# A decoder block in split float32: low parts a megabyte at a time, and the high-weight products first

## The chip, the core and the metric

The kernel runs on one core of a Trainium2 chip. A core has a matrix engine (TensorE, PE in the profile), a vector engine (VectorE, DVE), an activation engine (ScalarE, ACT), a general engine (GpSimd, POOL), and a queue engine (SyncE, SP) that issues the transfers; 16 DMA engines move data between the device memory and the on-chip memory. Matmul results land in accumulator banks, each 128 rows of 512 floats. The engines run apart from each other, each in the order of its own list, and meet at semaphores.

The metric is the device time of one execution in microseconds. The kernel before takes 1417.61 us (median of three runs, 1417.16 to 1417.9).

## The reference

One block of a decoder over 256 tokens of width 2048, in float32:

```
h    = rmsnorm(x, attn_norm_w)
proj = h @ w_in            # rq rk rv rg | mq mk mv | g_ret g_moba
o_ret  = retention(rotary(rq), rotary(rk), rv)     # 4 heads of 256, chunks of 128
o_ret  = silu(rg) * norm(o_ret) * ret_norm_w
o_moba = moba_attention(rotary(mq), rotary(mk), mv) # 8 heads of 128
merged = sigmoid(g_ret) * (o_ret @ w_ret_up) + sigmoid(g_moba) * (o_moba @ w_moba_up)
x  = x + merged @ w_out
h2 = rmsnorm(x, ffn_norm_w)
a, b = split(causal_conv3(h2 @ w_ffn_up))           # 2 x 5632 wide
x  = x + (silu(a) * b) @ w_ffn_down
out = rmsnorm(x, final_norm_w)
```

Nearly all of the work is in the products with weights.

## The kernel before, in words

**Numbers in two parts.** To be exact enough, each operand of a product is split into a high part, which is the number rounded to the format in which TensorE multiplies, and a low part, which is the rest. ScalarE writes the high part (L185, a copy that rounds), VectorE the low part (L186, the number less its high part). A product is then three matmuls: high by high, high by low and low by high (`mm3`, L196 to L199; every matmul is recorded by `mm`, L194).

**Slots.** The weights, some 264 MB, stream through the chip in halves of 512 KB (128 x 1024 floats, `raw`), each fetched by one transfer (`load`, L168) into one of RAW_BUFS = 4 buffers, and split by `part` into `whi` and `wlo`, PART_BUFS = 4 buffers each. Two halves are a slot, and there are 252 slots, numbered from 0 in the order in which TensorE goes through them: keys, queries, values and gates of the two attentions (0 to 55), the gates and the up products of both attentions, four columns of blocks with 12 slots each (56 to 103), the output product (104 to 119), the up projection of the feed-forward part (120 to 207) and its down projection in two passes of 22 slots (208 to 251).

**Three kinds of slot.** Keys, queries and the up projection are *wide*: the weights stand in the array and the tokens move through; a slot is 16 matmuls of 512 columns (high and low part of the tokens side by side, by the high part of the weights) and 16 of 256 columns (by the low part), in two rounds of two blocks of columns for keys, queries and the first up slots and in one round for the rest. The others are *plain*: 24 matmuls of 512 columns, three for each of eight products, or *seven*: a Strassen form with 21, in which four sums of weight blocks (VectorE) replace a product. Sums of token blocks for the seven slots are made by `seven_sums`: L748 to L752 on VectorE, a copy on ScalarE (L755), and the low part (L756). The tables SEVEN_GATES, SEVEN_OUT and SEVEN say which slots of a stage are seven slots.

**The order of the work.** There is no scheduler: the program is written slot by slot, and each engine's list is the order of the writing. At a slot: first the split of the next slot's weights (`part`, or the seven form), and with it the load of the slot that will use the freed buffers; then `seven_sums` where there is one; then one step of each task in hand (`run_tasks`: rotary, attention, gates, convolution, gathering of results); then the slot's matmuls (`issue`, L204), with the small matmuls and transposes of the tasks put into the middle of the stream. So what a task on VectorE or ScalarE needs stands in line behind the split of the next slot's weights.

**Places that the prediction names.** L629 is the gate of the retention attention, which reads an accumulator, on ScalarE; L846 multiplies products with the gates, from accumulators, on VectorE; L851 adds the output product to x (VectorE), which is then transposed on TensorE (L202) for the up projection; L541 is the convolution, L545 the silu `g` behind it (ScalarE) and L546 the product with the other branch. In the down projection `seven_parts` (first pass, sums written in place) and `seven_parts_apart` (second pass, sums in tiles `tt`, their parts in `th`, `tl` or `t`) split a seven slot.

Of the kernel before, what the change touches and what calls it, by code (L numbers as in the profile page):

```python
# [33 lines left out]
RAW_BUFS, PART_BUFS = 4, 4  # L34
# [45 lines left out]
SEVEN = ((4, 7, 10, 13, 16, 18), (3, 5, 7, 9, 12, 14, 16))  # L80
# [45 lines left out]
def block(ctx: ExitStack, tc: tile.TileContext, a):  # L126
# [15 lines left out]
    def f32(ap):  # L142
        return ap.bitcast(F32)
# [15 lines left out]
    def spans(n):  # L159
        step = CW if n < 1 else 2 * CW  # L160
        return [slice(c, c + step) for c in range(0, 2 * CW, step)]

    def load(n, *some):
        if n < n_halves:
            if n not in raws:
                raws[n] = wp.tile([P, 2 * CW], F32, name="raw", bufs=RAW_BUFS)
            for w in some or spans(n):
                nc.sync.dma_start(raws[n][:, w], wts[order[n], :, w])  # L168

    def part(n, *some):  # L170

        if n < n_halves:
            if n not in parts:
                parts[n] = [wp.tile([P, 2 * CW], F32R, name=x, bufs=PART_BUFS) for x in ("whi", "wlo")]
            for w in some or spans(n):
# [20 lines left out]
    def mm3(out, ah, al, bh, bl, start, stop, **kw):  # L196
        mm(out, ah, bh, start=start, stop=False, **kw)
        mm(out, ah, bl, start=False, stop=False, **kw)
        mm(out, al, bh, start=False, stop=stop, **kw)  # L199

# [72 lines left out]
    xtiles = [px.tile([P, 2, 2, S], F32R, name=f"xb{i}", bufs=1) for i in range(KD // 2)]  # L273
# [18 lines left out]
    def part_x(k):  # L292
        for j in range(k, min(k + 2, KD)):
            split2(xh[j], xl[j], xts[j // 4][:, j % 4, :], vec[:, V_ATTN + j:V_ATTN + j + 1])
            if k == 0:
                part(0, spans(0)[j])
# [230 lines left out]
    def ffn(acc, f):  # L527

        pf = big["pf"]
        u = big["u"][f % 2]  # L530
        y = pf.tile([P, 2, S], F32, name="y", bufs=2)
# [12 lines left out]
        g = pf.tile([P, S], F32, name="g", bufs=2)  # L544
# [72 lines left out]
    def closed(kind, n, acc, more):  # L617
# [17 lines left out]
        elif kind == "up":  # L635
            if n == 0:
# [4 lines left out]
                big["u"] = [pf.tile([P, 2, S + 2], F32, name=f"u{i}") for i in range(2)]  # L641
# [14 lines left out]
    load(0)  # L656
# [8 lines left out]
    part(1)  # L665
# [12 lines left out]
    def seven_parts(n):  # L678


        r, q = raws.pop(n), raws.pop(n + 1)
        b11, b21, b12, b22 = r[:, :CW], r[:, CW:], q[:, :CW], q[:, CW:]
        (h1, l1), (h2, l2) = [[wp.tile([P, 2 * CW], F32R, name=x, bufs=PART_BUFS) for x in ("whi", "wlo")]
                              for _ in range(2)]
        (h3, l3), t2 = big["t14"], big["t2"]
# [15 lines left out]
        for i in (0, 1):  # L701
            load(n + i + RAW_BUFS)
# [490 lines left out]
```

## Time and profile before

| | before |
|---|---|
| time, median of 3 runs | 1417.61 us |
| the profiled execution, first to last instruction (span) | 1415.7 us |
| TensorE busy | 1405.6 us (99%) |
| VectorE busy | 1103.4 us (78%) |
| ScalarE busy | 776.9 us (55%) |
| read from memory | 272.86 MB, 194 GB/s over the span |
| granted TensorE clock | 0.999 |

The span is measured inside the profiled execution; the times of the runs are some 2 us longer, since they hold what lies around it. In the timeline a row gives start, duration, engine, line, operation, what is written from what, and the shape; rows of the same kind that follow each other are joined (x2). Matmuls are pipelined: a row of 0.39 us may be followed by the next 0.23 us later, so the pace is read from starts, not from durations.

The chain that ended last has next to nothing in it: the last operations of the kernel and 0.3% of the span in which nothing was waited for.

### The profile page before, as it was taken

How to read it: one execution, taken by the hardware profiler on the slowest of the kernel's cores; microseconds unless marked ns; L12 is line 12 of the kernel's file. 1: busy time of each engine (PE TensorE's matmuls, PEld its weight loads, DVE VectorE, ACT ScalarE, POOL GpSimd, SP SyncE). 2: the span in 40 equal slices, each digit the busy share in tenths (PEclk: the TensorE clock that was granted, in tenths of full speed). 3: DMA queues.
4: the chain of work that ended last, by engine and by line, in shares of the span. 5: the costliest groups of instructions: out<-in, count | busy, mean ns of one | idle time of the engine just before them, and what ended most of it. 6: DMA issues, size and time to landing. Idle time of an engine off the chain costs nothing. (4 is left out here: it accounts for less than half of the span.)

```text
span 1415.7 us, 19297 instructions
## 1 busy us (share of the span) xinstructions
PE 1405.6 (99%) x7215; PEld 1202.7 (85%) x7215; DVE 1103.4 (78%) x1512; ACT 776.9 (55%) x1043; POOL 5.6 (0%) x14
## 2 busy tenths in 40 slices
PE   9999999999999999999999999999999999999997
PEld 7888888888888888888888888888888888888886
DVE  6687656867888989798677777777777778998886
ACT  6555454545556555555565555555555555555553
POOL 0000000000000000000000000000000000000000
PEclk9999999999999999999999999999999999999999
DMA  8755555555656656577555656556556555657664
GB/s 296 260 187 168 167 186 172 178 179 172 212 182 209 195 191 209 180 236 238 167 190 188 197 181 193 194 182 194 191 182 196 189 179 178 207 180 236 191 217 160
DMA packets 77325, 276.22 MB, mean 195 GB/s; under 512 B 8720, under 2 KB 9776, under 8 KB 77232
## 3 DMA queue, kind: packets, MB, share of 16 engines
q1 hardware_dynamic: 76800, 274.20, 60.1%
q8 instruction: 56, 0.92, 0.3%
q10 hardware_dynamic: 432, 0.79, 0.2%
q14 instruction: 37, 0.30, 0.1%
HBM read 272.86 MB, written 2.10 MB: 194 GB/s over the span
## 5 line engine op out<-in xcount | busy, mean ns | idle before, releaser
L186 DVE TENSOR_TENSOR wlo<-raw,whi 128x1024 fp32r<-128x1024 f32 (+1 forms) x493 | 584.1, 1219 | 234.7 <-ACT whi L185 108.8
L185 ACT ACTIVATE whi<-raw 128x1024 fp32r<-128x1024 f32 (+1 forms) x493 | 514.5, 1058 | 458.9 <-PE acc L194 247.9
L194 PE MATMUL acc<-xb,whi 128*128 128x512 f32 x1920 | 466.0, 392 | 1.1 <-ACT whi L185 1.1
L194 PEld LDWEIGHTS acc<-xb,whi 128*128 128x128 f32 x1920 | 350.6, 188 | 68.6 <-ACT whi L185 2.1
L194 PEld LDWEIGHTS acc<-xb,wlo 128*128 128x128 f32 x1920 | 250.9, 191 | 12.2
L194 PE MATMUL acc<-xb,wlo 128*128 128x256 f32 x1920 | 254.6, 282 | 0.0
L194 PE MATMUL acc<-whi,xb 128*128 128x512 f32 x572 | 183.3, 391 | 0.0
L194 PEld LDWEIGHTS acc<-whi,xb 128*128 128x128 f32 x572 | 107.4, 188 | 22.1
L194 PE MATMUL acc<-wlo,xb 128*128 128x512 f32 x286 | 111.5, 390 | 0.0
L194 PE MATMUL acc<-wlo,gh 128*128 128x512 f32 (+1 forms) x226 | 87.5, 387 | 0.0
L194 PE MATMUL acc<-whi,gl 128*128 128x512 f32 (+1 forms) x226 | 87.5, 387 | 0.0
L194 PE MATMUL acc<-whi,gh 128*128 128x512 f32 (+1 forms) x226 | 87.5, 387 | 0.0
L541 DVE SCALAR_TENSOR_TENSOR y<-u,vec,y 128x256 f32<-128x256 f32 x176 | 73.5, 479 | 0.0
L194 PEld LDWEIGHTS acc<-wlo,xb 128*128 128x128 f32 x286 | 53.7, 188 | 10.6
L194 PE MATMUL z<-whi,xb 128*128 128x512 f32 x156 | 51.9, 390 | 0.0
L194 PEld LDWEIGHTS acc<-wlo,gh 128*128 128x128 f32 x226 | 42.4, 188 | 8.8
L194 PEld LDWEIGHTS acc<-whi,gh 128*128 128x128 f32 x226 | 42.4, 188 | 8.7
L194 PEld LDWEIGHTS acc<-whi,gl 128*128 128x128 f32 x226 | 42.4, 188 | 8.6
L538 ACT ACTIVATE y<-u,vec 128x256 f32<-128x256 f32 x88 | 47.7, 590 | 0.0
L194 PEld LDWEIGHTS z<-whi,xb 128*128 128x128 f32 x156 | 29.3, 188 | 6.1
L755 ACT ACTIVATE s<-room 128x512 fp32r<-128x512 f32 x13 | 8.2, 633 | 44.7 <-DVE room L752 44.7
L534 DVE TENSOR_TENSOR u<-y,r2b 128x512 f32<-128x512 f32 x44 | 30.5, 693 | 1.5
(304 smaller groups left out, 1593.1 us busy)
## 6 DMA issues: line engine op xcount, KB each, us to landing
raw<-in_wts SPq DMA_DIRECT2D x503, 512.0 KB, 4.3
rows<-in_x SPq DMA_DIRECT2D x4, 512.0 KB, 7.7
x<-in_x SPq DMA_DIRECT2D x4, 512.0 KB, 6.1
xt<-in_xT SPq DMA_DIRECT2D x3, 512.0 KB, 7.0
wf<-in_wf SPq DMA_DIRECT2D x2, 512.0 KB, 7.1
out<-x SPq DMA_DIRECT2D x4, 256.0 KB, 2.5
out<-x ACTq DMA_DIRECT2D x2, 384.0 KB, 3.3
xt<-in_xT SPq DMA_DIRECT2D x2, 256.0 KB, 4.4
```

The costliest lines, as they stand in the source:

```text
L185: nc.scalar.activation(hi, full, AF.Copy)
L186: nc.vector.tensor_sub(lo, full, f32(hi))
L194: to.append(lambda: nc.tensor.matmul(out, a, b, **kw))
L534: nc.vector.tensor_mul(u[:, :, 2:], y, twice(big["r2b"]))
L538: nc.scalar.activation(y[:, j, :], u[:, j, 0:S], AF.Identity, scale=cv[j][:, 0:1], bias=cv[j][:, 3:4])
L541: nc.vector.scalar_tensor_tensor(y[:, j, :], u[:, j, i:i + S], cv[j][:, i:i + 1], y[:, j, :], op0=OP.mult, op1=OP.add)
L755: nc.scalar.activation(hi, sums, AF.Copy)
```

## The change

1. **Buffers of a slot.** `raw`, `whi` and `wlo` become tiles of a whole slot (128 x 2048), two of each. ScalarE still writes the high parts in two copies of 128 x 1024, but VectorE makes the low parts of the slot in one operation (`part`). Both loads of the slot after next go out when that operation is done. The first three slots are still split half by half (`part_of`).
2. **Order within a slot.** In plain and seven slots `all3` writes first, for every product, high by high and low by high, the two that use the high part of the weights; then, for every product, the one that uses their low part.
3. **One form of the seven slots.** `seven_parts` replaces both old forms. Another variant of the Strassen form is used, with other signs and another order of products; the four sums are made ahead, three of them in `tt`; one subtraction of 128 x 2048 makes the low parts of the slot, and one of 128 x 1536 those of the three sums. In the down projection `tt` lies in a tile `uy` which also holds the up projection's u, y and g of the last tasks. The first seven slot of the first pass moves from the fifth to the sixth place (SEVEN 4 to 5: slot 212 to 213).
4. **Keys and queries** are described as going in two halves of a slot with two blocks of columns each; the calls of `wide_products` have other text and the same arguments for every slot.

```diff
-RAW_BUFS, PART_BUFS = 4, 4
+RAW_BUFS, PART_BUFS = 2, 2
...
-SEVEN = ((4, 7, 10, 13, 16, 18), (3, 5, 7, 9, 12, 14, 16))
+SEVEN = ((5, 7, 10, 13, 16, 18), (3, 5, 7, 9, 12, 14, 16))
...
-    def part(n, *some):
-
-        if n < n_halves:
-            if n not in parts:
-                parts[n] = [wp.tile([P, 2 * CW], F32R, name=x, bufs=PART_BUFS) for x in ("whi", "wlo")]
-            for w in some or spans(n):
-                split2(parts[n][0][:, w], parts[n][1][:, w], raws[n][:, w])
-            if not some or some[0] == spans(n)[-1]:
-                raws.pop(n)
-                load(n + RAW_BUFS)
...
+    def loads(s):
+        raws.pop(s)
+        for h in range(2):
+            load(2 * (s + RAW_BUFS) + h)
...
+    def part(s):
+
+        if 2 * s < n_halves:
+            hi, lo = parts[s] = part_tiles()
+            for h in range(2):
+                w = slice(2 * CW * h, 2 * CW * (h + 1))
+                nc.scalar.activation(hi[:, w], raws[s][:, w], AF.Copy)
+            nc.vector.tensor_sub(lo, raws[s], f32(hi))
+            loads(s)
...
+    def all3(products):
+
+        for bank, edges, ah, al, bh, bl in products:
+            for x in (ah, al):
+                begin, end = edges(1)
+                mm(bank, x, bh, start=begin, stop=end, to=stream)
+        for bank, edges, ah, al, bh, bl in products:
+            begin, end = edges(1)
+            mm(bank, ah, bl, start=begin, stop=end, to=stream)
...
+                uy = big["uy"] = pf.tile([P, 8 * S + 2 * S + 8], F32, name="uy")
+                y1, u1, u0, y0, g = [uy[:, w:w + n] for w, n in ((0, 2 * S), (2 * S, 2 * S + 4), (4 * S + 4, 2 * S + 4),
+                                                                 (6 * S + 8, 2 * S), (8 * S + 8, 2 * S))]
...
+    def seven_parts(s, tt, th, tl):
+
+        r = raws[s]
+        b11, b21, b12, b22 = [r[:, x * CW:(x + 1) * CW] for x in range(4)]
+        hi, lo = parts[s] = part_tiles()
+        nc.vector.tensor_sub(tt[0], b22, b21)
+        nc.vector.tensor_sub(b22, b22, b12)
+        nc.vector.tensor_sub(tt[1], b12, tt[0])
+        nc.vector.tensor_sub(tt[2], b11, tt[1])
+        for h in range(2):
+            w = slice(2 * CW * h, 2 * CW * (h + 1))
+            nc.scalar.activation(hi[:, w], r[:, w], AF.Copy)
...
+            full = tt[3]
+            nc.scalar.activation(th, full, AF.Copy)
+            nc.vector.tensor_sub(lo, r, f32(hi))
+            nc.vector.tensor_sub(tl, full, f32(th))
+        loads(s)
...
-        for key, (ah, al), (bh, bl) in (
-                ("e0", a(0, 0), b(0, 0)), ((0, 0), a(0, 1), b(0, 1)), ((0, 1), ss[3], b(1, 1)),
-                ("e3", ss[2], b(1, 0)), ("e2", ss[1], t2), ("e1", ss[0], t1), ((1, 0), a(1, 1), t4)):
-            begin, end = accs.edges(key, 3)
-            mm3(accs.bank(key), ah, al, bh, bl, begin, end, to=stream)
+        all3([(accs.bank(key), functools.partial(accs.edges, key), *x, *y) for key, x, y in (
+            ("e0", a(0, 1), b(0, 1)), ((0, 0), a(0, 0), b(0, 0)), ((0, 1), ss[3], b(1, 0)), ("e3", ss[2], b(1, 1)),
+            ("e1", ss[0], t1), ("e2", ss[1], t2), ((1, 0), a(1, 0), t4))])
...
+        full = big["uy"][:, 4 * S + 4:4 * S + 4 + 3 * CW].rearrange("p (x t) -> p x t", x=3)
+        tt = three(full) + [full]
...
-            elif slot < 3:
+            if slot < 3:
                 for h in range(2):
                     wide_products(accs, 4 * kc + 2 * h, halves[h:h + 1], nk, range(4))
             else:
-                for blocks in ((0, 1), (2, 3)):
+                for blocks in (range(4),) if kind == "up" and n > 0 else ((0, 1), (2, 3)):
                     wide_products(accs, 4 * kc, halves, nk, blocks)
```

What this does to the engines' lists, at the three places of which the prediction speaks. First TensorE at slot 56, the first slot of the gates stage; xb is the token block, acc an accumulator. Before, its beginning:

```order
L194 MATMUL acc<-whi,xb_80 128x512
L194 MATMUL acc<-wlo,xb_80 128x512
L194 MATMUL acc<-whi,xb_80 128x512 x2
L194 MATMUL acc<-wlo,xb_80 128x512
L194 MATMUL acc<-whi,xb_80 128x512 x2
```

and now the whole slot:

```order
L215 MATMUL acc<-whi,xb_80 128x512 x16
L215 MATMUL acc<-wlo,xb_80 128x512 x8
```

The eight matmuls with the low part of the weights moved from every third place to the end, and the slot's second accumulator, with which its twelfth matmul (counted from 0) used to begin, is now begun by its eighth.

Second VectorE around the same slot: the split of slot 56, the token sums (L748 to L756 before, L773 to L781 now), and the split of slot 57. Before:

```order
L186 TENSOR_TENSOR wlo<-raw,whi 128x1024 x2
L748 TENSOR_TENSOR room<-xb_80 128x512
L749 TENSOR_TENSOR room<-room 128x128
L750 TENSOR_TENSOR room<-room 128x128
L751 TENSOR_TENSOR room<-room 128x128
L752 TENSOR_TENSOR room<-room 128x128
L756 TENSOR_TENSOR s_3194<-room,s_3194 128x512
L186 TENSOR_TENSOR wlo<-raw,whi 128x1024 x2
```

and now:

```order
L196 TENSOR_TENSOR wlo<-raw,whi 128x2048
L773 TENSOR_TENSOR room<-xb_80 128x512
L774 TENSOR_TENSOR room<-room 128x128
L775 TENSOR_TENSOR room<-room 128x128
L776 TENSOR_TENSOR room<-room 128x128
L777 TENSOR_TENSOR room<-room 128x128
L781 TENSOR_TENSOR s_2966<-room,s_2966 128x512
L196 TENSOR_TENSOR wlo<-raw,whi 128x2048
```

The list is the same but for the two operations that became one ahead of the sums and behind them. Slot 120, the first of the up projection, has the same exchange ahead of the four additions of L851, and its matmuls keep their order.

Third VectorE from the split of slot 212 to that of slot 215, now (gl is the low part of the activations, L583 the convolution, L588 the product behind the silu, t the low parts of the sums):

```order
L196 TENSOR_TENSOR wlo<-raw,whi 128x2048
L207 TENSOR_TENSOR gl<-uy,gh 128x256
L583 SCALAR_TENSOR_TENSOR uy<-uy,vec 128x256 x4
L729 TENSOR_TENSOR uy<-raw 128x512
L730 TENSOR_TENSOR raw<-raw 128x512
L731 TENSOR_TENSOR uy<-raw,uy 128x512
L732 TENSOR_TENSOR uy<-raw,uy 128x512
L745 TENSOR_TENSOR wlo<-raw,whi 128x2048
L746 TENSOR_TENSOR t<-uy,t 128x1536
L588 TENSOR_TENSOR uy<-uy 128x256
L196 TENSOR_TENSOR wlo<-raw,whi 128x2048
L773 TENSOR_TENSOR room<-otrh,otrl 128x512
```

Before, the convolution stood behind the split of the first seven slot (212), and the split of slot 213 and the sums followed it. Now it stands ahead of the first seven split (213); that split's sums are written into the tile uy, which the silu behind the convolution writes too, and the sums of tokens follow with slot 214.

More of the change, by code (lines that the diff above doesn't have):

```diff
@@ L1 @@
+import functools
 from contextlib import ExitStack
@@ L199, in mm3, with counted, edges @@
         mm(out, al, bh, start=False, stop=stop, **kw)
+    def counted(n):
+        left = [n]
+        def edges(some):
+            begin = left[0] == n
+            left[0] -= some
+            return begin, left[0] == 0
+        return edges
+    def all3(products):
[6 more added lines that the diff above has]
+            mm(bank, ah, bl, start=begin, stop=end, to=stream)
     def flip(out, full):
@@ L727, in two_blocks, with three @@
+    def three(tile, w=CW):
+        return [tile[:, x, :] for x in range(3)]
     def two_blocks(k, kind="dn"):
@@ L780, in plain_products @@
                 w = slice(kk * CW, (kk + 1) * CW)
[L781 to L784 removed]
+                some += [(accs.bank((t, j)), functools.partial(accs.edges, (t, j)),
+                          *(x[:, kk, t * P:(t + 1) * P] for x in xs), hi[:, w], lo[:, w]) for t in range(NT)]
+        all3(some)
     class Banks:
@@ L902, in middle_slots @@
                 middle_pool()
-                t124 = [[big[x][:, i, :] for x in ("th", "tl")] for i in range(3)]
-            n = 2 * (slot + 1)
+                th, tl = big["th"], big["tl"]
+                t124 = list(zip(three(th), three(tl)))
             if q == 0 and seven:
@@ L946, in middle_slots @@
             run_tasks()
-            halves = [parts.pop(2 * slot + h) for h in range(2)]
+            halves = halves_of(slot)
             if seven:
@@ L1027, in down_slots @@
                 weighted(2, 1)
-            halves = [parts.pop(2 * slot + h) for h in range(2)]
+            halves = halves_of(slot)
             if seven:
@@ L1062, in down_slots, with products @@
                     spawn(added, tiles[0][d], d)
-    def products(kind, n, act, accs, kc, halves, tokens, nk):
+    def products(kind, n, act, accs, kc, halves, counts, nk):
         if len(accs) == 4:
-            if kind == "up" and n > 0:
-                wide_products(accs, 4 * kc, halves, nk, range(4))
-            elif slot < 3:
+            if slot < 3:
                 for h in range(2):
@@ L1111, in block @@
             run_tasks()
-            halves = [parts.pop(2 * slot + h) for h in range(2)]
-            products(kind, n, act, accs, kc, halves, range(NT), nk)
+            halves = halves_of(slot)
+            products(kind, n, act, accs, kc, halves, counts, nk)
             issue()
```

153 lines of the change are left out of this document (63 added, 90 removed).

## The prediction

> **What bounds the kernel now.** I read the page's parts 1 and 2 first, then the waits of TensorE, then its timeline around every tight place.
>
> ```profile
> PE 1405.6 (99%) x7215; PEld 1202.7 (85%) x7215; DVE 1103.4 (78%) x1512; ACT 776.9 (55%) x1043; POOL 5.6 (0%) x14
> PE   9999999999999999999999999999999999999997
> PEclk9999999999999999999999999999999999999999
> ...
> PE idle L651 <- DVE idle L648: 1.2, 1, 1.2
> PE acc L194 <- ACT whi L185: 1.1, 1, 1.1
> ```
>
> TensorE is busy for 99% at full clock and waits 2.3 us in all, both times in the first 10 us. So the time is the number of matmuls times their pace, plus what little it stands. The pace stands in the timeline of TensorE, here the start of slot 56, whose second matmul is at 341.17 (so its first, number 0, at 340.94):
>
> ```profile
> 341.17 0.39 PE L194 MATMUL acc<-wlo,xb 128*128 128x512 f32 x1
> ...
> 342.76 0.62 PE L194 MATMUL acc<-whi,xb 128*128 128x512 f32 x2
> 343.21 0.39 PE L194 MATMUL acc<-wlo,xb 128*128 128x512 f32 x1
> 343.44 0.62 PE L194 MATMUL acc<-whi,xb 128*128 128x512 f32 x2
> ```
>
> From wlo to wlo, three matmuls, is 0.68 us: 0.227 us each. A plain slot (24) takes 5.44 us, a seven slot (21) 4.76. The change issues the same matmuls in the same sizes, so work on TensorE cannot shrink; only new or lost standstills can move the time.
>
> **Part by part.** *One subtraction instead of two.* The groups by form give the two-half price; a 128x2048 subtraction isn't there, and the nearest row is the 128x2048 product of L978.
>
> ```profile
> L186 DVE TENSOR_TENSOR wlo<-raw,whi 128x1024 fp32r<-128x1024 f32 x491 | 582.7, 1221 | 234.6 <-ACT whi L185 108.8 <-PE acc L194 71.7 <-issue 53.1
> L185 ACT ACTIVATE whi<-raw 128x1024 fp32r<-128x1024 f32 x491 | 513.3, 1059 | 458.9 <-PE acc L194 247.9 <-issue 111.0 <-DVE raw L716 38.1
> 1394.55 2.29 DVE L978 TENSOR_TENSOR x<-x,wf 128x2048 f32<-128x2048 f32 x1
> ```
>
> I take 2.29 us; the bounds are that and the two back to back, 2.36. Up to 0.16 us (2 x 1.221 - 2.29) of VectorE is saved per slot, some 38 us over 248 slots, on an engine that TensorE does not wait for: worth nothing. What it costs is lateness. The first half's low parts used to begin when ScalarE had that half's high parts; now they wait for both halves, about 1 us more. Behind the waiting subtraction stand VectorE's later operations, in order, and then whoever waits for those.
>
> The Trainium skill (Perfetto Trace Analysis, section "Optimizing Scalar/DVE Operations") says that grouping operations can help where the engine is saturated, and that where Vector is not, but makes bubbles elsewhere, breaking instructions up may let work complete sooner. That speaks against this edit: VectorE is busy 78% here. By the grouping half the 38 us would be a gain; by the other half, the sum below has the right sign.
>
> *Two buffers of a slot for four of a half.* In the long stage of the up projection:
>
> ```profile
> 1114.55 2.36 DVE L186 TENSOR_TENSOR wlo<-raw,whi 128x1024 fp32r<-128x1024 f32 x2 [1.54 <-PE acc L194]
> ...
> 1115.25 3.82 PE L194 MATMUL acc<-xb,whi 128*128 128x512 f32 x16
> ...
> 1120.81 0.63 PE L194 MATMUL acc<-xb,whi 128*128 128x512 f32 x2
> ```
>
> The low parts of the slot that starts at 1120.81 were done at 1116.9. Now their buffer comes free when the slot before last ends, at 1115.25; they end near 1117.8, and are first read behind 16 matmuls, 3.6 us into the slot. That leaves over 6 us: nothing is lost. Loads go out about 1 us later, with the same cover. At the start the DMA engines are full (418 GB/s from 12 to 14 us, the last column of the windows), so a later issue only queues later:
>
> ```profile
> 12.00:14.00 2.00, 2.00 (x15) 1.78 (x14) 1.51 (x2) 2.00 (x4) 0.00 (x0) 1.00 1.05 418
> ```
>
> *Order within plain and seven slots.* The high-weight products come first, so a low part is due at matmul 16 (3.6 us) or 14 (3.2 us) and no longer at 1. But a slot's second accumulator is now first written by matmul 8, no longer 12: 0.91 us earlier. *Keys and queries:* the calls give the same order as before, no effect.
>
> Now the places where these meet something late.
>
> *Slot 56*, first of the gates. The accumulator that matmul 12 (343.66) starts was read by the gate operations of L629.
>
> ```profile
> 337.40 2.36 DVE L186 TENSOR_TENSOR wlo<-raw,whi 128x1024 fp32r<-128x1024 f32 x2 [0.78 <-ACT whi L185]
> 339.68 0.68 DVE L748 TENSOR_TENSOR room<-xb 128x512 f32<-128x512 f32 x1
> ...
> 341.12 0.29 DVE L752 TENSOR_TENSOR room<-room 128x128 f32<-128x128 f32 x1
> ...
> 336.29 2.02 ACT L185 ACTIVATE whi<-raw 128x1024 fp32r<-128x1024 f32 x2
> 341.45 0.63 ACT L755 ACTIVATE s<-room 128x512 fp32r<-128x512 f32 x1 [3.14 <-DVE room L752]
> 341.99 1.25 ACT L629 ACTIVATE gate<-acc,r 128x512 f32<-128x512 f32 x2
> ```
>
> The gates ended at 343.24, 0.42 us early. Now: high parts ready 338.31, subtraction to 340.64 (was 339.76), 0.88 us later for the sums (to 342.29), for s, and for the gates: 344.12. With 0.17 us that the slot before adds in the same way, 344.3. Matmul 8 is due at 342.76. Standstill **1.5 us** (bounds 1.1, if ScalarE's copies, whose buffers come free sooner, make up the lateness; 1.8).
>
> *Slot 120*, first of the up projection.
>
> ```profile
> 682.45 3.89 ACT L185 ACTIVATE whi<-raw 128x1024 fp32r<-128x1024 f32 x4
> ...
> 683.53 2.36 DVE L186 TENSOR_TENSOR wlo<-raw,whi 128x1024 fp32r<-128x1024 f32 x2 [0.46 <-ACT whi L185]
> 685.81 2.48 DVE L851 TENSOR_TENSOR x<-z,x 128x512 f32<-128x512 f32 x4
> ...
> 684.37 1.98 PE L194 MATMUL acc<-xb,whi 128*128 128x512 f32 x8
> 686.18 1.11 PE L194 MATMUL acc<-xb,wlo 128*128 128x256 f32 x8
> 687.13 1.03 PE L202 MATMUL z<-ident,x 128*128 128x128 f32 x8
> ```
>
> Two of the four copies end at 684.45. The subtraction runs from 684.49 to 686.78, but this kind of slot keeps its order and reads low parts at 686.18: 0.6 us. The four additions of L851 then start 0.85 us late; the second transpose, which stands right behind the second of them (687.1), adds 0.15. **0.75 us** (bounds 0.5 and 0.95).
>
> *Slot 215*, second seven slot of the down projection; the first moves from 212 to 213, so the two are nearer, and the sums of blocks (tt) now share a tile with the last activations g.
>
> ```profile
> 1199.82 1.67 DVE L541 SCALAR_TENSOR_TENSOR y<-u,vec,y 128x256 f32<-128x256 f32 x4
> ...
> 1205.99 0.40 ACT L545 ACTIVATE g<-y 128x256 f32<-128x256 f32 x1
> ...
> 1214.02 0.39 PE L194 MATMUL acc<-whi,otrh 128*128 128x512 f32 x1
> ...
> L186 DVE TENSOR_TENSOR tl<-tt,th 128x1536 fp32r<-128x1536 f32 x16 | 28.0, 1752 | 0.2 <-ACT th L185 0.2
> L185 ACT ACTIVATE th<-tt 128x1536 fp32r<-128x1536 f32 x16 | 23.8, 1489 | 2.5 <-DVE tt L718 2.4
> ```
>
> I walk it with these durations. In the new order the convolution (L541) stands behind the subtraction of 212 and ahead of the four sums of 213, and can end near 1197.6; its last low part, 1.75 us, ends near 1204.3. Until then g's silu may not write; behind it ScalarE has the copies of 214 (1204.7 to 1206.7), then VectorE that subtraction (to 1209.0), the sums of L748 with s and gl (3.4 us, to 1212.4), the four sums for 215 (4 x 0.69, the 512-wide price of L748, to 1215.2) and ScalarE the copy th (1.49, to 1216.7). Slot 215 starts 0.1 us earlier than the row, 1213.9, and reads th at matmul 8, 1215.7. **1.0 us** (bounds 0, if the convolution or the loads let the chain start 1 us sooner, and 1.3).
>
> *What is won.* One short standstill of the old in-place form goes:
>
> ```profile
> 1273.85 1.77 PE L194 MATMUL acc<-t,s 128*128 128x512 f32 x6
> 1275.47 0.62 PE L194 MATMUL acc<-t,otmh 128*128 128x512 f32 x2
> ...
> 1273.62 1.22 DVE L699 TENSOR_TENSOR t<-raw,t 128x1024 fp32r<-128x1024 f32 x1
> ```
>
> Six matmuls should take 1.36 us and took 1.62; part of t landed at 1274.84. The new form ends with one 1.75 us operation for t and its turn is 6.8 us of VectorE (four sums, 2.29, 1.75) in a slot pair that has 10. **-0.25 us** (bounds 0, -0.25).
>
> *Left at nothing:*
>
> ```profile
> 406.02 0.39 PE L194 MATMUL z<-whi,xb 128*128 128x512 f32 x1
> ...
> 406.22 1.29 DVE L846 TENSOR_TENSOR sr<-acc,sr 128x512 f32<-128x512 f32 x2 [0.72 <-PE acc L194]
> ...
> 1396.76 2.51 DVE L186 TENSOR_TENSOR wlo<-raw,whi 128x1024 fp32r<-128x1024 f32 x2
> ...
> 1399.69 0.39 PE L194 MATMUL acc<-wlo,gh 128*128 128x512 f32 x1
> ```
>
> Slot 68 (and 80 alike) starts at 406.02; L846 frees an accumulator at 407.51, and matmul 8 now writes it at 406.02 + 1.82 = 407.84: 0.3 us of cover. The last subtraction ends at 1399.27, 0.4 us before it is read, in an order that stays. Cover gone, each costs some 0.3 us.
>
> Sum: 1.5 + 0.75 + 1.0 - 0.25 = **+3.0 us**. The profiled span is 1415.7 us, the runs' median 1417.61, 1.9 above it; so 1418.7 in a profile and **1420.6** in runs.
>
> **The rivals.**
>
> *The lateness is absorbed.* ScalarE's buffers of high parts come free after matmul 16 of a slot, and its copies could run enough ahead. For it: ScalarE is busy 55%. Against it: at 56 and 120 the row shows the copies held by their place behind other work, not by buffers. Only the 0.25 us remain: 1417.4.
>
> *Matmul pairs go faster.* Plain and seven slots now put two matmuls with the same moving weights back to back. There are 132 such slots (252 less 120 of the wide kind) with some 3,070 matmuls. If that let each start 1 ns sooner, 3.1 us go: 1417.5; from 2 ns on it decides (6.1 us: 1414.5). Against it: slots of 16 equal-operand matmuls, 1115.25 to 1118.90 above, pace at 0.228 us, no faster than alternating ones. The Trainium skill (TensorE: Matmul & The Clock Gate, "Back-to-back issue gap") gives 216 ns for an isolated gap at 512 columns and 131 sustained; the rows here show 227 in every order, so neither is reached. By 216 ns at 3,070 matmuls the sum would be some 33 us lower, an estimate from that page.
>
> *Starved slots.* Each load waits for a whole slot's split, and a late weight would stop TensorE in many slots. Price: 0.1 us in each of the 88 up slots is 8.8 us: 1429. It decides only where the 6 us of cover worked out above vanish, and nothing in the rows shows a landing that late.
>
> **How the numbers follow.** A measurement here can tell about 0.2%, 2.8 us, from no change. Forecast with its standstills, 0.73; absorbed, 0.14; faster pairs, 0.07; starved, 0.06. The forecast's own bounds are 1.1 + 0.5 + 0 - 0.25 = 1.35 and 1.8 + 0.95 + 1.3 = 4.05, with 0.6 for the places left at nothing: 1419.0 to 1422.3, on both sides of 1420.45; I give 0.45 of it to slower and 0.28 to no change. So slower 0.51, same 0.42, faster 0.07. The range 1417.0 to 1423.5 takes in most of the absorbed case and a place that I missed.
>
> **What would show it.** In the changed profile, waits of TensorE on the gate (near 343), on a 128x2048 wlo (near 688) and on t (near 1218), of 1.5, 0.6 and 1 us; none near 1277. The pace of 0.227 us unchanged. VectorE's busy time about 40 us lower with the span no shorter. It is wrong if those waits are missing, if waits come elsewhere, or if the matmuls' pace differs.

## The result: 11 us slower, and the profile after

| | before | changed |
|---|---|---|
| time, median of the runs | 1417.65 us | 1428.74 us (4 runs, 1428.42 to 1429.04) |
| ratio to the kernel before | | 1.0080 [1.0066, 1.0094] |
| span of the profiled execution | 1415.7 us | 1427.1 us |
| granted TensorE clock | 0.999 | 0.998 |

The forecast was 1420.6 us, +3.0, with a range to 1423.5. The kernel lost 11.1 us: the sign was right, the size was not, and the time lies outside the range.

The page of the changed kernel, its engines (busy time, share of the span, instructions), and the waits of TensorE (its line, engine and line it waited for: us in all, times, longest):

```profile
PE 1409.0 (99%) x7215; PEld 1202.8 (84%) x7215; DVE 1081.7 (76%) x1238; ACT 756.2 (53%) x1017; POOL 5.6 (0%) x14
...
PE acc L215 <- DVE mfull L408: 2.2, 3, 1.1
PE acc L215 <- ACT gate L671: 1.6, 1, 1.6
PE idle L697 <- DVE idle L694: 1.2, 1, 1.2
PE z L215 <- DVE mgl L207: 1.1, 1, 1.1
PE acc L243 <- issue: 0.9, 1, 0.9
PE acc L215 <- DVE wlo L196: 0.9, 1, 0.9
PE acc L215 <- ACT whi L206: 0.7, 1, 0.7
PE acc L215 <- ACT t L744: 0.7, 2, 0.4
PE acc L215 <- DVE rfull L408: 0.5, 2, 0.3
PE z L243 <- DVE sr L943: 0.2, 1, 0.2
```

The same 7215 matmuls ran. Before, TensorE waited for two things, both in the first 10 us; now there are ten lines, of which idle and whi are the old two. Three of the others were forecast (gate, wlo, t). The largest, mfull, was not, nor were mgl, the "issue" of L243, rfull and sr. VectorE is 21.7 us less busy, and it bought nothing.

The groups by form tell where VectorE stands instead (instructions, busy us, mean ns of one; then the idle time of the engine ahead of them and what ended it):

```profile
L196 DVE TENSOR_TENSOR wlo<-raw,whi 128x2048 fp32r<-128x2048 f32 x217 | 496.9, 2290 | 269.8 <-ACT whi L195 267.0 <-PE z L215 1.6 <-PE acc L215 1.2
```

The one subtraction takes 2.29 us, as taken from L978. But ahead of it VectorE waits 267.0 us for ScalarE's high parts; before, the row of L186 had 108.8 us of that. Its other waits in that row before, 71.7 us for TensorE and 53.1 of "issue", have shrunk to 2.8 us: a wait for a whole slot's high parts has taken their place.

**Where the 11 us lie.** From each profile I took the time from a slot's first matmul to the next slot's, and subtracted. The table has the places that changed by 0.1 us or more; the first slot, which differs from execution to execution, is in the last row but one. "Ahead of slot 4" is time lost at the end of slot 3, with some 0.1 us in slot 4; the same goes for the others that say "ahead". The last two columns are experiments told below, in which the split of a slot is two subtractions again: in A each begins when its own half is ready, in B both wait for both halves.

| place | TensorE there waits for | forecast | changed | A | B |
|---|---|---|---|---|---|
| ahead of slot 4 | mfull (keys and queries, from the accumulators) | 0 | +1.76 | +0.20 | +1.28 |
| ahead of 9 and 12 | mfull | 0 | +0.90 | +0.11 | +1.76 |
| ahead of 16 | mfull | 0 | +0.78 | 0 | +0.79 |
| ahead of 44 and 48 | rfull (the same, retention) | 0 | +1.12 | 0 | +1.30 |
| in 56 | gate | +1.5 | +1.93 | +0.71 | +2.20 |
| 105 to 107 | sr, then mgl (merged, low part) | 0 | +1.82 | 0 | +1.63 |
| 118 | x, for its transposes | 0 | +1.09 | 0 | +1.57 |
| 120 | wlo | +0.75 | +1.23 | 0 | +1.36 |
| 215 | t | +1.0 | +0.73 | 0 | +0.86 |
| 226 | t | -0.25 | +0.28 | -0.27 | +0.67 |
| all the rest together (212 and 213, where the seven slot moved, cancel) | | 0 | -0.42 | -0.14 | -0.08 |
| sum | | +3.0 | +11.2 | +0.6 | +13.3 |

Of the 11.2 us, 3.9 lie at the three places that were forecast to stand (3.25 forecast), and about 7.5 at places counted as nothing. (B loses another 1 us behind the start of its last slot, which the table leaves out.)

**A forecast place.** Slot 56 in the timeline of the changed kernel (start, duration, engine and line, operation; in brackets the idle time before and what ended it):

```profile
340.98 2.02 ACT L195 ACTIVATE whi<-raw 128x1024 fp32r<-128x1024 f32 x2
347.02 0.63 ACT L780 ACTIVATE s<-room 128x512 fp32r<-128x512 f32 x1 [4.02 <-DVE room L777]
347.55 1.25 ACT L671 ACTIVATE gate<-acc,r 128x512 f32<-128x512 f32 x2
...
343.03 2.29 DVE L196 TENSOR_TENSOR wlo<-raw,whi 128x2048 fp32r<-128x2048 f32 x1 [1.72 <-ACT whi L195]
346.69 0.29 DVE L777 TENSOR_TENSOR room<-room 128x128 f32<-128x128 f32 x1
...
339.81 3.79 PE L215 MATMUL acc<-whi,xb 128*128 128x512 f32 x16
343.44 1.98 PE L215 MATMUL acc<-wlo,xb 128*128 128x512 f32 x8
345.25 1.98 PE L215 MATMUL acc<-whi,xb 128*128 128x512 f32 x8
348.85 1.43 PE L215 MATMUL acc<-whi,xb 128*128 128x512 f32 x5 [1.63 <-ACT gate L671]
```

The chain is the forecast one: copies, the late subtraction, the sums, s, the gates, and matmul 8, due at 345.25 + 1.82 = 347.07, is issued at 348.85. One link was short. The copies begin 4.27 us ahead of the slot; before they began 4.65 ahead (336.29, slot at 340.94). So 0.38 us of lateness came in from earlier slots, of which the forecast had 0.17. The rows of TensorE also settle the pace: 16 matmuls in pairs on the same moving weights from 339.81 to 343.44 are 0.227 us each, as before.

**A place that was not forecast.** Slots 105 to 107, changed kernel:

```profile
605.18 1.99 ACT L195 ACTIVATE whi<-raw 128x1024 fp32r<-128x1024 f32 x2
...
607.21 2.29 DVE L196 TENSOR_TENSOR wlo<-raw,whi 128x2048 fp32r<-128x2048 f32 x1 [1.21 <-ACT whi L195]
615.10 0.69 DVE L729 TENSOR_TENSOR tt<-raw 128x512 f32<-128x512 f32 x1 [0.94 <-DMA raw<-in_wts]
621.64 1.28 DVE L207 TENSOR_TENSOR mgl<-z,mgh 128x512 fp32r<-128x512 f32 x2
...
609.53 5.46 SPq L170 DMA_DIRECT2D raw<-in_wts  x4
...
622.37 0.50 PE L215 MATMUL z<-whi,mgh 128*128 128x512 f32 x1 [1.07 <-DVE mgl L207]
```

and the same two VectorE operations before:

```profile
598.89 2.36 DVE L186 TENSOR_TENSOR wlo<-raw,whi 128x1024 fp32r<-128x1024 f32 x2 [0.26 <-ACT whi L185]
605.90 0.68 DVE L715 TENSOR_TENSOR tt<-raw 128x512 f32<-128x512 f32 x1
```

Before, the subtraction of slot 105 (which began at 602.82) ended 1.6 us ahead of the slot. Now it ends at 609.50, 0.6 us into the slot (608.90). The loads of slot 107 go out behind it, from 609.53 on, the second lands at 615.0, and VectorE stands 0.94 us for them; before, the first sum of 107 began without a wait and 3.3 us ahead of slot 106 (609.16), now 0.6 us ahead (615.70). The sums, the subtraction, the low parts of the sums and then mgl, all on VectorE, come too late for slot 107's first matmuls. This is the late load that the prediction put at nothing, in a chain of two slots, and the subtraction of slot 105 came late into it.

Slot 118 is alike, changed kernel:

```profile
673.44 2.23 ACT L195 ACTIVATE whi<-raw 128x1024 fp32r<-128x1024 f32 x2 [2.57 <-DMA raw<-in_wts]
...
675.71 2.29 DVE L196 TENSOR_TENSOR wlo<-raw,whi 128x2048 fp32r<-128x2048 f32 x1 [2.24 <-ACT whi L195]
682.61 0.69 DVE L850 TENSOR_TENSOR x<-acc,x 128x512 f32<-128x512 f32 x1
...
683.40 1.94 PE L243 MATMUL acc<-ident,x 128*128 128x128 f32 x16 [0.89 <-issue]
```

ScalarE waits 2.57 us for late weights, whose loads went out behind the subtraction of slot 116, VectorE 2.24 us for both copies, the eight operations that gather the output product (L842 to L850) stand behind them, and the transposes of x wait. The profile says "issue" for that wait; the row of L850, which ends at 683.30, shows what it was. Before, the last of the same eight operations ended 1.1 us into the slot (671.72), now 3.7 us into it (679.63):

```profile
672.14 0.69 DVE L827 TENSOR_TENSOR x<-acc,x 128x512 f32<-128x512 f32 x1
```

**The start**, changed kernel, then before:

```profile
25.74 2.22 ACT L195 ACTIVATE whi<-raw 128x1024 fp32r<-128x1024 f32 x2 [0.90 <-DMA raw<-in_wts]
...
27.99 2.29 DVE L196 TENSOR_TENSOR wlo<-raw,whi 128x2048 fp32r<-128x2048 f32 x1 [1.72 <-ACT whi L195]
30.20 1.28 DVE L408 TENSOR_TENSOR mfull<-acc,mfull 128x512 f32<-128x512 f32 x2
...
30.94 3.25 PE L215 MATMUL acc<-whi,xb 128*128 128x512 f32 x13 [1.08 <-DVE mfull L408]
```

```profile
25.47 1.23 DVE L186 TENSOR_TENSOR wlo<-raw,whi 128x1024 fp32r<-128x1024 f32 x1 [0.89 <-ACT whi L185]
27.62 0.69 DVE L365 TENSOR_TENSOR mfull<-acc,mfull 128x512 f32<-128x512 f32 x1 [0.92 <-ACT mfull L364]
```

mfull frees an accumulator that slot 4 begins with. VectorE used to stand idle for 0.92 us ahead of it; now it is queued behind a subtraction that ends at 30.28.

### The profile page after: what moved, and what is told of

It reads as the page before. It is cut to its first block, busy times and chain, and to the rows that moved or that the text cites. A ratio compares the mean times of both kernels' runs of the same rounds, so it can differ in the third digit from the quotient of the medians.

```text
span 1427.1 us, 18529 instructions
## 1 busy us (share of the span) xinstructions
PE 1409.0 (99%) x7215; PEld 1202.8 (84%) x7215; DVE 1081.7 (76%) x1238; ACT 756.2 (53%) x1017; POOL 5.6 (0%) x14
## 5 line engine op out<-in xcount | busy, mean ns | idle before, releaser
L196 DVE TENSOR_TENSOR wlo<-raw,whi 128x2048 fp32r<-128x2048 f32 x217 | 496.9, 2290 | 269.8 <-ACT whi L195 267.0
L195 ACT ACTIVATE whi<-raw 128x1024 fp32r<-128x1024 f32 x434 | 436.5, 1051 | 369.5 <-PE acc L215 232.4
L215 PE MATMUL acc<-whi,xb 128*128 128x512 f32 x572 | 142.0, 392 | 3.4 <-ACT gate L671 1.6
L735 ACT ACTIVATE whi<-raw 128x1024 fp32r<-128x1024 f32 x62 | 65.6, 1060 | 106.8 <-DVE raw L730 51.3
L215 PE MATMUL acc<-wlo,xb 128*128 128x512 f32 x286 | 73.5, 390 | 0.0
L583 DVE SCALAR_TENSOR_TENSOR uy<-uy,vec 128x256 f32<-128x256 f32 x176 | 73.3, 479 | 0.0
L745 DVE TENSOR_TENSOR wlo<-raw,whi 128x2048 fp32r<-128x2048 f32 x29 | 66.3, 2285 | 0.4 <-ACT whi L735 0.4
L215 PE MATMUL acc<-wlo,gh 128*128 128x512 f32 (+1 forms) x226 | 57.9, 387 | 0.0
L580 ACT ACTIVATE uy<-uy,vec 128x256 f32<-128x256 f32 x88 | 47.6, 589 | 0.4 <-DVE uy L576 0.4
L215 PE MATMUL z<-whi,xb 128*128 128x512 f32 x156 | 39.6, 389 | 0.0
```

The lines of the kernel that those rows point to most:

```text
L195: nc.scalar.activation(hi[:, w], raws[s][:, w], AF.Copy)
L196: nc.vector.tensor_sub(lo, raws[s], f32(hi))
L215: to.append(lambda: nc.tensor.matmul(out, a, b, **kw))
L580: nc.scalar.activation(y[:, j, :], u[:, j, 0:S], AF.Identity, scale=cv[j][:, 0:1], bias=cv[j][:, 3:4])
L583: nc.vector.scalar_tensor_tensor(y[:, j, :], u[:, j, i:i + S], cv[j][:, i:i + 1], y[:, j, :], op0=OP.mult, op1=OP.add)
L735: nc.scalar.activation(hi[:, w], r[:, w], AF.Copy)
```

## The experiments

The theories: the loss comes from the **wait** of the one subtraction for both halves (S in the expectations), or from the **loads** and buffers of a whole slot (L); later, whether the long up stage has a part in it, and whether each place pays for its own late subtraction or for lateness **carried** in over several slots (C). The expectations name more theories and say what each is; their theories A and B are not the experiments A and B of the table. Edits are shown against the changed kernel, shortened, but for the order alone, which is an edit of the kernel before. Times are medians, compared with the kernel before as run beside them (1417.1 to 1417.4 us).

### Two subtractions again, all else as changed (A)

```diff
-            nc.vector.tensor_sub(lo, raws[s], f32(hi))
+                nc.vector.tensor_sub(lo[:, w], raws[s][:, w], f32(hi[:, w]))
             loads(s)
```

and the same in `seven_parts`, but for the two seven slots of the first column.

> The changed kernel with the low parts of a slot again in two subtractions of 128x1024, each right behind the high parts of its half; buffers of a slot and loads (both behind the second subtraction) stay as changed. Theory S (the one subtraction, which waits for both high halves, makes the lateness): most of the 11.1 us returns, 1419 to 1421, with the stands at slots 56 and 120 down from 1.9 and 1.2 us to under 0.8 each. Theory L (the loads, which go out a slot at a time and later, make it): 1426 to 1428, the stands ahead of slots 4, 106 and 118 stay within 0.3 us.

Measured: 1418.28 us, ratio 1.0007 [0.9998, 1.0017]. Some 10.2 of the 11.1 us are gone, with whole-slot buffers, the loads of a slot still issued together behind the second subtraction, the new order and the new seven form all kept. The wait theory stands; the buffers alone cannot be the cause. What is left in the profile is slot 56 (0.71 us), and the win of 0.27 us at 226 is there. The group of the subtraction:

```profile
L196 DVE TENSOR_TENSOR wlo<-raw,whi 128x1024 fp32r<-128x1024 f32 x434 | 512.1, 1221 | 239.2 <-ACT whi L195 143.5 <-PE acc L215 88.8 <-issue 4.2
```

### Two subtractions, but both behind both copies (B)

The same number of operations as in A, with the second half first, so that the first of them needs the last copy.

```diff
-            nc.vector.tensor_sub(lo, raws[s], f32(hi))
+            for h in (1, 0):
+                w = slice(2 * CW * h, 2 * CW * (h + 1))
+                nc.vector.tensor_sub(lo[:, w], raws[s][:, w], f32(hi[:, w]))
             loads(s)
```

> The changed kernel with two subtractions of 128x1024 in plain and wide slots, that of the second half first, so that both wait for both high copies; nothing else changed. Theory W (the wait for both copies is the cost, not the size of the operation): as the changed kernel or a little more, 1428 to 1431. Theory B (one long operation as such is the cost): 1419 to 1421.

Measured: 1432.41 us, ratio 1.0110 [1.0095, 1.0126], with stands at the places of the changed kernel (column B of the table) and one more ahead of slot 9. The group:

```profile
L198 DVE TENSOR_TENSOR wlo<-raw,whi 128x1024 fp32r<-128x1024 f32 x434 | 511.7, 1220 | 261.5 <-ACT whi L195 261.0
```

Between A and B lie some 14 us. Both have two operations of 1.22 us in the plain and wide slots; they differ in what those wait for there (143.5 against 261.0 us for ScalarE; in the seven slots B keeps the one subtraction, and A's two come behind both copies as well). The seven slots cannot make the difference: in the changed kernel their subtraction waits 0.4 us for the copies over 29 of them together. So the price is that of the wait, not of the size. Given the wait, one operation is the better form: B is some 4 us above the changed kernel (1.0110 and 1.0080 of the kernel before, intervals that just don't meet).

### Loads by halves as well

Buffers of raw weights by halves, each loaded again as soon as its own subtraction is done; high and low parts still in whole-slot tiles; two subtractions.

```diff
-RAW_BUFS, PART_BUFS = 2, 2
+RAW_BUFS, PART_BUFS = 4, 2
...
-            nc.vector.tensor_sub(lo, raws[s], f32(hi))
-            loads(s)
+                nc.vector.tensor_sub(lo[:, w], raws[2 * s + h], f32(hi[:, w]))
+                loads(2 * s + h)
```

> As the run with two subtractions, and the weights land again in four buffers of a half, each reloaded behind its own subtraction; high and low parts stay in two buffers of a slot. Theory L: the stands ahead of slots 4, 106 and 118 (1.6, 1.2 and 1.1 us) go, and the time is 4 us or more under the run with two subtractions alone: 1418 to 1421. Theory S: within 1 us of that run.

Measured: 1417.76 us, ratio 1.0003 [0.9993, 1.0012]. Beside A, 0.5 us, no more than such a comparison can tell. With two subtractions the later load is covered, as the prediction had it; slot 56 keeps its 0.71 us.

### The order alone, and the old order with one subtraction

The kernel before with the new order in plain and seven slots:

```diff
-                for t in range(NT):
-                    begin, end = accs.edges((t, j), 3)
-                    mm3(accs.bank((t, j)), *(x[:, kk, t * P:(t + 1) * P] for x in xs), hi[:, w], lo[:, w],
-                        begin, end, to=stream)
+                some += [(accs.bank((t, j)), functools.partial(accs.edges, (t, j)),
+                          *(x[:, kk, t * P:(t + 1) * P] for x in xs), hi[:, w], lo[:, w]) for t in range(NT)]
+        all3(some)
```

(and likewise in the other two places).

> The kernel before with only the new order of the products in plain and seven slots; buffers of halves, both old forms of the seven slots. Theories S and L: the order costs little by itself, 0.5 us at slot 56 where an accumulator is begun 0.91 us sooner, less the 0.25 us of slot 226: 1417.5 to 1418.5. Theory O (the order makes the loss, by accumulators that are begun sooner and finished later): over 1422. Were matmul pairs faster, under 1416.

Measured: 1416.66 us, ratio 0.9995 [0.9986, 1.0005]: no change that can be told. The stand of some 0.5 us at slot 56 that I expected, from matmul 8 in place of 12, did not come. Its timeline there:

```profile
335.24 2.02 ACT L186 ACTIVATE whi<-raw 128x1024 fp32r<-128x1024 f32 x2
340.95 1.27 ACT L650 ACTIVATE gate<-acc,r 128x512 f32<-128x512 f32 x2
...
340.75 3.79 PE L195 MATMUL acc<-whi,xb 128*128 128x512 f32 x16
```

In the new order the high parts of both halves have been read after two thirds of the slot, and ScalarE's copies run 5.51 us ahead of slot 56, where they ran 4.65 ahead before. The gates end at 342.22 and matmul 8 is due at 342.57. So the order brings its own cover for what it takes, if the parts are buffered by halves; with tiles of a whole slot (A) the 0.71 us stay.

The changed kernel with its three matmuls of a product together, as before:

```diff
-            for x in (ah, al):
-                begin, end = edges(1)
-                mm(bank, x, bh, start=begin, stop=end, to=stream)
-        for bank, edges, ah, al, bh, bl in products:
-            begin, end = edges(1)
-            mm(bank, ah, bl, start=begin, stop=end, to=stream)
+            begin, end = edges(3)
+            mm3(bank, ah, al, bh, bl, begin, end, to=stream)
```

> The changed kernel with three matmuls of a product behind each other again; buffers, one subtraction and the new form of the seven slots stay. Theories S and L: low parts are late and now read by matmul 1 of a slot: slower than the changed kernel, some 4 us (1432 to 1434), most of it in the first pass of the down projection (slots 214 to 228, whose low parts end up to 3 us behind the slot's start). Theory O: back to 1418 to 1421.

Measured: 1457.0 us, ratio 1.0284 [1.0267, 1.0301]. The sign is as expected, the size a miss: +39.6 where some +15 was expected. The waits of TensorE:

```profile
PE acc L215 <- DVE wlo L196: 9.4, 10, 1.5
PE acc L215 <- DVE wlo L741: 7.8, 7, 2.5
```

So TensorE waits for low parts themselves, 17 times in these two lines: in this order they are due at the second matmul. The new order is worth nothing measurable to the kernel before and 28 us to the kernel with one late subtraction: it is what makes that subtraction bearable at all.

### One subtraction in one stretch at a time

Two subtractions everywhere but in a range of slots (in `part`, and in `seven_parts` where the range has seven slots):

```diff
+                if not 121 <= s < 208:
+                    nc.vector.tensor_sub(lo[:, w], raws[s][:, w], f32(hi[:, w]))
+            if 121 <= s < 208:
+                nc.vector.tensor_sub(lo, raws[s], f32(hi))
```

First the up projection, 87 slots:

> The run with two subtractions, but with the one subtraction of 128x2048 in the 87 slots 121 to 207 of the up projection, where low parts have 6 us of cover. Theory Q (the one subtraction costs only where something short of cover stands behind it on VectorE): 1418.3, within 1 us of the run with two. Theory A (each one costs something, a share of the 10.5 us by slots: 87 of 246): 1421 to 1422.

Measured: 1418.16 us, ratio 1.0007 [0.9998, 1.0016], the same as A. No slot of that stage differs. That is what theory Q gave. The rival of starved slots, which was priced on this stage, falls, and the prediction's 6 us of cover there stand.

The output product and the first up slot, 104 to 120:

> The run with two subtractions, but with one subtraction in slots 104 to 120 alone. Theory Q with places that add up: the stands of the changed kernel there (0.45, 1.23, 1.09 and 1.23 us at 105, 106, 118 and 120, with 0.3 around them) come back and no others: 1418.3 + 4.1 = 1422.4, within 0.7. If lateness is mostly carried in from earlier slots: 1419 to 1420.5.

Measured: 1420.55 us, ratio 1.0025 [1.0016, 1.0035], less than expected. Slots 118 (+1.01) and 120 (+1.23) stand again. Slots 105 and 106, which have the one subtraction here too, do not. So these two do not stand for their own subtraction alone. That asked for the stretch that ends there, 96 to 107:

> The run with two subtractions, but with one subtraction in slots 96 to 107 alone. In the run with one in 104 to 120 the stands at 105 and 106 did not come back. Theory C (they are lateness carried in over several slots, each subtraction behind the last one's followers): with eight more slots ahead they come back, 0.45 + 1.2 us: 1419.5 to 1420.2. Rival (they need the whole program before them, or were chance): under 0.3 us at both, 1418.0 to 1418.6.

Measured: 1420.02 us, ratio 1.0018 [1.0009, 1.0028]. 105 (+0.45), 106 (+0.83 of 1.23) and 107 (+0.14) stand again. The lateness is made in part before the output product (up to slot 103) and paid in 105 to 107: it is carried. The subtraction of slot 105 shows how much. In A it ends 1.52 us ahead of the slot; with the one subtraction from 104 on 0.61 ahead, which the slot bears; with it from 96 on 0.59 behind the slot's start, and in the changed kernel 0.60. So 0.9 us are made there and 1.2 come in, and in the traces of the last two the lateness builds up from slot 102 on. The profiled execution (1421.14 us, 1.1 above its median) also stands 1.23 us ahead of slot 4, in a stretch with two subtractions, on weights that landed late:

```profile
27.04 2.20 ACT L195 ACTIVATE whi<-raw 128x1024 fp32r<-128x1024 f32 x2 [2.35 <-DMA raw<-in_wts]
```

So the whole-slot loads do cost something at the start in some executions. The four other profiles with two subtractions in slot 4 and whole-slot loads lose 0.1 us at most at the end of slot 3. How much of the 1.8 us ahead of slot 4 is the loads' in the changed kernel, these runs do not tell.

The projections and the first gates, 4 to 60:

> The run with two subtractions, but with one subtraction in slots 4 to 60 alone. If the places add up, the stands of the changed kernel in this part come back and no others: ahead of slots 4, 12, 16, 44, 48 (1.4, 0.8, 0.6, 0.4, 0.4, with 0.1 beside each) and 1.9 at 56, of which 0.7 stands already: 1423 to 1424. If the lateness needs long trains of slots, less than half of it: under 1421.

Measured: 1423.11 us, ratio 1.0039 [1.0025, 1.0052]. Every stand of the changed kernel in that stretch is back in its size (slot 3 +1.47 and 56 +1.91, where it had +1.65 and +1.93; 11, 15, 43 and 47, the slots ahead of 12, 16, 44 and 48, within 0.02), and none elsewhere. Ahead of these four nothing is carried: ScalarE's copies begin at the same point in A and in the changed kernel (0.70 or 0.75 us ahead of the slot in which they stand), and the subtraction ends 0.8 to 0.9 us later. And slot 4 is the first of all with one subtraction.

The first half of the down projection, 208 to 229:

> The run with two subtractions, but with one subtraction in slots 208 to 229, the first pass of the down projection, alone. Theory C: the up projection ahead has cover, so nothing is carried in, and the stands of the changed kernel at 215 and 226 (0.7, and 0.55 where the run with two has none) come back: 1418.3 + 1.3 = 1419.6, within 0.5. Rival (they were carried in from before the up projection): 1418.0 to 1418.6.

Measured: 1419.84 us, ratio 1.0017 [1.0008, 1.0027], as expected. Slots 215 (+0.70) and 226 (+0.24) stand again.

The five stretches, each above the kernel before and less A's own +0.93, are 4.8 (4 to 60), 1.7 (96 to 107), 2.5 (104 to 120), 0.1 (up) and 1.6 (208 to 229): 10.7 us, and with A's 0.9 some 11.6 beside the changed kernel's 11.1. The stretches leave out 61 to 95 and 230 to 251, where no slot of the changed kernel is 0.1 us longer. The places add up within what these comparisons can tell, 1.3 to 1.9 us either way for each.

### The subtraction behind the tasks

If what stands behind the subtraction is late, put the subtraction behind it: one subtraction, and the loads, after `run_tasks`.

```diff
-            nc.vector.tensor_sub(lo, raws[s], f32(hi))
-            loads(s)
+            later.append(lambda: (nc.vector.tensor_sub(lo, r, f32(hi)), loads(s)))
...
             run_tasks()
+            low()
```

> The changed kernel with the one subtraction of plain and wide slots (and the loads behind it) put behind the slot's tasks and token sums in VectorE's list, no longer ahead of them; seven slots as changed. Theory Q (who stands behind the subtraction is what counts, since low parts themselves have time until matmul 16): most of the loss returns, 1417 to 1421. Rival (low parts or loads are late in themselves): 1427 or more.

Measured: 1440.51 us, ratio 1.0164 [1.0149, 1.0180]; the expectation missed. The stands ahead of 44 and 48, in 56 and at 105 are gone, but new ones came, of 4.2 us (slot 41) and 4.1 (slot 45), and some 7 us in the first pass of the down projection. The waits of TensorE, and slot 41 in the timeline:

```profile
PE acc L222 <- DVE wlo L204: 10.4, 11, 2.7
```

```profile
255.99 2.28 DVE L204 TENSOR_TENSOR wlo<-raw,whi 128x2048 fp32r<-128x2048 f32 x1
...
258.32 2.07 PE L222 MATMUL acc<-xb,wlo 128*128 128x256 f32 x8 [2.67 <-DVE wlo L204]
```

Now the rotary work stands ahead of the subtraction, and the low parts are late. VectorE's wait for the copies fell to 45.4 us here (its group's row), and the kernel is the slowest but one: the engine's waiting time is not the price; what counts is whether each result is there when it is due.

### The order and the new seven form, buffers by halves, two subtractions

> The changed kernel with all buffers of halves (weights as landed, high parts and low parts, four each) and two subtractions; the order of products and the new form of the seven slots stay. The stand of 0.7 us at slot 56, which the run with two subtractions keeps and the run of the order alone does not have, should go if it is the buffers of high and low parts by slots that make it: 1416.5 to 1417.3. Rival (the new form of the seven slots makes it): 1417.5 to 1418.3.

```diff
-RAW_BUFS, PART_BUFS = 2, 2
+RAW_BUFS, PART_BUFS = 4, 4
...
-            nc.vector.tensor_sub(lo, raws[s], f32(hi))
-            loads(s)
+                split2(*parts[s][h], raws[2 * s + h])
+                loads(2 * s + h)
```

Measured: 1416.43 us, ratio 0.9993 [0.9984, 1.0002]. No stand at 56 any more, so the 0.71 us there come from whole-slot tiles of the parts beside the new order (with raw halves alone they stayed). The traces show the way: in A the subtraction of slot 55 begins at 330.63, behind a wait of 1.62 us for TensorE, just after slot 53 has ended (330.37) and its tile of low parts is free; here it begins at 328.81, behind one of 0.70 us, and the copies of slot 56 behind it run 5.51 us ahead of the slot, in A 4.60. It is the lowest median of all, but its interval reaches no change; I do not call it faster.

## Why the prediction was wrong in size

**The pace and what bounds the kernel: right.** The same matmuls at 0.227 us; TensorE bound, only stands matter. The faster-pairs rival falls with it.

**The one subtraction: its duration right, its saving overstated, its cost located too narrowly.** 2.29 us as taken. Of the 38 us of busy time VectorE saved 21.7. The 38 were made from two durations of 1.221, though the rows say that two back to back take 2.36 together: 248 x 0.07 is 17, most of what was saved. It made no difference, since that time was worth nothing.

**The step that failed** is "Now the places where these meet something late": a list of three places to stand and three left at nothing, each priced with the lateness of its own slot (0.88 us, and 0.17 from the slot before). Two things in it were wrong, and together they make the 7.5 us that I had not priced.

The list was too short. The wait is in every slot, and I had looked at six of them. Ahead of 4, 9 and 12, 16, 44 and 48, mfull or rfull stands behind the subtraction and frees an accumulator that the next slot begins with. These places cost 4.6 us and had little slack: ahead of 12, 16, 44 and 48 (2.8 us with slot 9) the lateness of one subtraction, 0.8 to 0.9 us, made slots 0.4 to 0.8 us longer, with nothing carried in. Ahead of 4 the loads may have a share.

The price was too low where lateness is carried. VectorE's small operations stand behind the subtraction, ScalarE's (s, gate) behind those, ScalarE's next copies behind these, and the next subtraction behind the copies; the load of the slot after next is issued behind the subtraction. In a stretch of slots with little slack the lateness goes from slot to slot until a result is due. That made the other 2.9 us: sr and mgl in 105 to 107, where the subtraction was 2.1 us later than in A, and x in 118, where the copies begin 1.0 us later than in A and the subtraction ends 1.9 us later. Restricting the one subtraction to stretches showed it for 105 and 106: they stood when slots 96 to 107 had it, and not when 104 to 120 had it. For 118 it is read from the trace alone.

**Two buffers of a slot for four of a half, "nothing is lost":** right in the up stage, for which it was worked out. At slot 56 the whole-slot tiles of the parts take away the cover that the new order brings, 0.71 us with two subtractions.

**"Loads go out about 1 us later, with the same cover":** right in the up stage and with two subtractions (A, and loads by halves beside it). Wrong together with a late subtraction: the first sum of slot 107 began 2.7 us later against the slots, and for 0.94 us of that VectorE stood for the weights. "A later issue only queues later" was wrong at the start in at least one execution. The starved-slots rival so had a real mechanism, late weights, and the wrong place and price. That its 1429 lies next to the measured time is chance: of the 88 up slots only 120 stands, and that for low parts.

**The three forecast stands:** the chains are those of the prediction. 56 stood 1.93 us for 1.5, and 120 stood 1.23 for 0.75; both take up 0.4 us that the copies were late already (at 120 they begin 1.53 us ahead of the slot, before 1.92). 215 stood 0.73 for 1.0. Together 3.9 for 3.25; 56 and 120 lie above their bounds (1.8 and 0.95).

**226, "what is won":** wrong. It stands 0.28 us more, not 0.25 less. I walked the chain of sums, subtraction, tokens' sums and copy for 215 and not for 226, where the same list is:

```profile
1274.62 2.29 DVE L196 TENSOR_TENSOR wlo<-raw,whi 128x2048 fp32r<-128x2048 f32 x1
1279.88 0.69 DVE L729 TENSOR_TENSOR uy<-raw 128x512 f32<-128x512 f32 x1
...
1282.73 1.49 ACT L744 ACTIVATE t<-uy 128x1536 fp32r<-128x1536 f32 x1 [0.35 <-DVE uy L732]
...
1284.28 1.20 PE L215 MATMUL acc<-t,s 128*128 128x512 f32 x4 [0.23 <-ACT t L744]
```

"6.8 us of VectorE in a slot pair that has 10" counted work, not the order it stands in. With two subtractions the 0.27 us are won, as forecast.

**Left at nothing** (68, 80, the last subtraction): right, nothing there. **Keys and queries described as halves:** no effect of the text; but their slots were where the subtraction hurt most, 4.6 us over the places ahead of 4, 9 and 12, 16, 44 and 48. **The absorbed rival** fell: ScalarE's copies did not make up the lateness in the changed kernel; in the order-alone run, where the parts are buffered by halves, they did make up for the accumulator that is begun sooner.

The Trainium skill (Perfetto Trace Analysis, section "Optimizing Scalar/DVE Operations") speaks for breaking up instructions where Vector is not saturated but makes bubbles elsewhere. The runs agree: with VectorE 76% busy, going back to two subtractions gave 10.2 us back. They add a condition: two that both wait for the last copy lose some 4 us more than one.

## What to carry to other kernels

Before two operations on an engine that does not bound the time are merged, ask what each of them waited for: if the inputs come one after the other, the merged one takes the later start of the two, in every turn of the loop, and hands it to all that stands behind it. Price that along the loop of engines that feed each other (here ScalarE's copies, VectorE, the load, ScalarE again), over several turns and up to each due time, and at every place where an engine waits for something behind the merged operation, not at the few that look tight; at slot 105 the subtraction came 2.1 us late, 1.2 of it from earlier turns, and its own 0.9 the slot would have borne. And an order of matmuls that makes late operands bearable should be judged together with what makes them late: here it was worth nothing alone and 28 us beside it.

## What the runs showed of the machine that I had not expected

Two VectorE subtractions back to back overlap: 1.221 us each in the group, 2.36 for the pair in the timeline, so one large operation saves 0.07 us of the engine and not 0.15. And an engine's standing says little of the time: ahead of the subtractions of weights VectorE stood 35 us longer than before (269.8 us in the changed kernel's row for 234.6 in that of before) where the kernel lost 11, and the run in which it stood least there, 45.5 us, with the subtraction behind the tasks, was some 12 us above the changed kernel.
